# Splitting the second attention's weights once, in the first feed-forward network, and fetching the parts from DRAM twice

## The chip, the cores and the metric

The kernel runs on one core of a Trainium2 chip. The metric is the time of one execution on the device in microseconds (us); the number compared is the median over runs.

## What is computed

Two transformer blocks, the output of the first being the input of the second. The change touches the second block alone, which works on L = 512 + 16 rows (16 "meta" rows) of width 1024:

```python
for layer in range(DEPTH_2):                      # 2 layers
    h = rms_norm_2(hs, norm_mix_pre[layer])
    if layer < N_A_LAYERS:
        mix = pool_mixer(h, pool_w[layer], pool_scale[layer])
    else:
        mix = sliding_window_attention(h, k_blk, v_blk, w_q[j], b_q[j], w_o[j], b_o[j], ...)
    hs = hs + rms_norm_2(mix, norm_mix_post[layer])
    h = rms_norm_2(hs, norm_ffn_pre[layer])
    hs = hs + rms_norm_2(swiglu(h, w_gate_up[layer], w_down[layer]), norm_ffn_post[layer])
    if layer == N_A_LAYERS - 1:
        kv_in = rms_norm_2(hs, kv_norm)
        k = kv_in @ w_k + b_k;  v = kv_in @ w_v + b_v
```

So the order of the work is: pooling mixer, first network (`swiglu`, hidden width 2816), attention with `w_k`, `w_v`, `w_q`, `w_o`, second network. All is float32.

## The kernel before, in words

Everything described here is in the class `Rest`, which runs the end of the first block and all of the second, and in `Stream`, which brings its weights. TensorE (PE) takes float32r operands. To keep float32 accuracy each weight and each activation is split in two float32r parts, hi (the rounded value) and lo (the remainder), and each product is three matmuls: hi by hi, hi by lo, lo by hi (`Net.mm3`). Activations are split once, where they are made.

Weights are split on the way. `Stream.plan` (method `Rest.plan`) lists them in the order of use as *units* of 128 x 2048 values (1 MB). `Stream.load` issues a unit's DMA on SP's queue into one of RAW = 2 buffers `raw`. `Stream.conv` makes *parts* of 128 x 1024 values of it: ScalarE (ACT) writes `whi`, VectorE (DVE) then `wlo`, into rings of RING = 4 buffers each. For `w_q`, `w_k` and `w_v` both instructions multiply by a norm's gain (`gq`, `gkv`). `take` hands the next part to the matmuls, `free` gives its place in the ring back, and `pump` then queues what has become possible: a load when the unit two before it is wholly converted, a conversion when fewer than 4 parts are between it and the oldest one in use.

```python
    RING, RAW = 4, 2
            if u < len(self.units) and (u < self.RAW or self.left[u - self.RAW] == 0):
                self.todo.append((None, None, lambda u=u: self.load(u)))
            elif j < len(self.order) and self.order[j][0] < u and j - self.n_free < self.RING:
                self.todo += self.conv(j)
```

The instruction order on every engine is fixed when the program is built. `Clock` reckons when each engine would be free; `Rest.turn` puts *sides* (generators such as `heads`, one for 128 queries and 4 heads of the attention) between the matmuls of the *main* sequence where the reckoned clock has passed their due time. Where `Clock` reckons that PE waits over 0.5 us for an operand, `Engine.warm` (line 1219) puts transposes of the identity in front, one for each 0.214 us of the reckoned wait. Each engine executes its queue in order.

The main sequence around the change: `up` and `down` of the first network alternate over hidden columns, in groups of 8, 8 and 6 tiles of 128. `down(f0, f1)` takes 8 parts, one for 128 output columns (below: a *column step*), and runs the matmuls of two row halves (256 and 272) on it. The last group runs `down` twice, once for each row half, and its weights are loaded twice. Then `kv` and `q` run for rows 256 and up, then for rows 0 to 255, so `w_k`, `w_v` (0.5 MB each) and `w_q` (4 MB) are loaded and split twice. `o_proj` runs for tiles 3 and 2, then for 0 and 1, and takes `w_o` (4 MB) each time in two halves of 4 parts. For tiles 0 and 1 it waits (`until`) for all their `heads`, of which at most two are under way.

Of the kernel before, what the change touches and what calls it, by code (L numbers as in the profile page):

```python
# [11 lines left out]
F32 = mybir.dt.float32  # L12
F32R = mybir.dt.float32r
# [7 lines left out]
P = 128  # L21
# [3 lines left out]
KC = D // P  # L25
# [6 lines left out]
U = 2048  # L32
# [17 lines left out]
class Rows:  # L50


    def __init__(self, net, ats):
        self.net, self.nc, self.ats = net, net.nc, ats
# [1220 lines left out]
class Stream:  # L1275
# [3 lines left out]
    def __init__(self, net, nc, clock):  # L1279
        self.net, self.nc, self.pool, self.clock = net, nc, net.wp, clock  # L1280
        self.units, self.order = [], []
        self.raw, self.left, self.live, self.ready = {}, {}, {}, {}
        self.todo = deque()
        self.n_load = self.n_conv = self.n_take = self.n_free = self.low = 0

# [16 lines left out]
    def add(self, *units):  # L1302

        for i in range(max(len(u) for u in units)):
            self.order += [u[i] for u in units if i < len(u)]

    def pump(self):

        while True:
            u, j = self.n_load, self.n_conv  # L1310
            if u < len(self.units) and (u < self.RAW or self.left[u - self.RAW] == 0):
                self.todo.append((None, None, lambda u=u: self.load(u)))
                self.n_load += 1
            elif j < len(self.order) and self.order[j][0] < u and j - self.n_free < self.RING:
                self.left[self.order[j][0]] -= 1
                self.todo += self.conv(j)
                self.n_conv += 1
            else:
                break
# [59 lines left out]

    def take(self, n):  # L1380
        out = []
        for _ in range(n):
            while self.n_take not in self.live:
                self.tick(1)
            out.append(self.live[self.n_take])
            self.n_take += 1
        return out

# [7 lines left out]
class Rest:  # L1396
# [463 lines left out]
        if keys:  # L1860
            self.until(*keys)

    def plan_down(self, lay, f0, f1):
        wdn = self.a["w_down"][lay].rearrange("(fc p) n -> p fc n", p=P)
        for dq in range(4):
            self.st.add(self.st.unit(wdn[:, f0:f1, 256 * dq:256 * dq + 256], f1 - f0, 256, "col"))

    def down(self, f0, f1, cols, act, yT, first):
        for c in range(KC):
# [101 lines left out]

        return at

    def plan_kv(self):
        for nm in ("w_k", "w_v"):
            self.st.add(self.st.unit(self.a[nm].rearrange("(kc p) n -> p kc n", p=P), KC, P, fix=self.scaled("gkv")(0)))

    def plan_q(self):
        wq = self.a["w_q"].rearrange("(kc p) n -> p kc n", p=P)
        for u in range(4):  # L1980
            self.st.add(self.st.unit(wq[:, :, 256 * u:256 * u + 256], KC, 256, fix=self.scaled("gq")(0)))

    def window_consts(self):
        nc, a = self.nc, self.a
# [180 lines left out]
    def plan(self):  # L2165
        self.plan_rows(self.a["w_ple_gate"], self.scaled("gp"))
        for lay, plan_down in ((0, self.plan_down), (1, self.plan_down_tokens)):
            for f in (0, 2, 0, 2, 4, 6):
                self.plan_up(lay, f)
            plan_down(lay, 0, 8)  # L2170
            for f0, f1 in self.groups:
                for f in range(f0, f1, 2):
                    self.plan_up(lay, f)
                plan_down(lay, f0, f1)
            if lay == 0:
                self.plan_down(0, 16, 22)
                for i in range(2):
                    self.plan_kv()
                    self.plan_q()
                for i in range(2):  # L2180
                    self.plan_rows(self.a["w_o_2"])

    def run(self, y2, proj):
        nc, a, net, st = self.nc, self.a, self.net, self.st
# [196 lines left out]
```

## Time and profile before

| | us |
|---|---|
| median of 3 runs | 1947.39 (1944.37 to 1947.91) |
| the profiled execution | 1945.09 |
| its span (first to last instruction) | 1943.3 |
| PE busy in it | 1890.7 (97%) |
| DVE busy, ACT busy | 813.4, 662.9 |

The span is what the views of the trace divide up; 1.8 us of the execution's time lie around it. PE's matmuls are pipelined, so "busy" does not mean that it runs at its peak rate. PEclk is the clock granted to TensorE as a share of its upper level of 2.4 GHz; 0.50 is the lower level, 1.2 GHz. SPq is SP's queue, which issues the DMAs; an issue's time to landing is from its issue to its last byte.

### The profile page before, as it was taken

What the parts mean: (1) busy time and instruction counts of PE and PEld (TensorE: products, weight loads), DVE (VectorE), ACT (ScalarE), POOL (GpSimd) and SP (SyncE); (2) the same over time, 40 slices, a digit from 0 to 9 for tenths busy, and PEclk for the clock granted to TensorE, in tenths of its full rate; (3) what the DMA queues carried; (4) which work ended last, traced back from release to release, by engine and by line L of the source; (5) the groups of instructions that cost most, each with busy time, mean ns of one, the idle gap of its engine ahead of it and who ended that gap; (6) DMA issues with size and microseconds to landing.
All of it is one profiled execution on the core that took longest, in us unless ns stands there. A gap on an engine that the chain in (4) does not pass through costs nothing.

```text
span 1943.3 us, 27812 instructions
## 1 busy us (share of the span) xinstructions
PE 1890.7 (97%) x11322; PEld 1473.8 (76%) x11322; DVE 813.4 (42%) x1740; ACT 662.9 (34%) x1394; POOL 107.1 (6%) x183
## 2 busy tenths in 40 slices
PE   9998999999999999988999999999999899999998
PEld 7766888855445445437899999999987598888886
DVE  5577334411111111118565323334897774233334
ACT  4333333221111111116464333223787663333232
POOL 2100000020000000001101000000100000000000
PEclk9999999999999999999999999999999899999999
DMA  7222236589999999995035322223433144223322
GB/s 191 87 87 65 85 103 238 215 356 384 417 417 417 418 417 417 419 400 212 23 109 178 110 94 88 87 88 98 146 126 109 66 157 158 87 90 106 108 76 76
DMA packets 182101, 365.58 MB, mean 188 GB/s; under 512 B 25909, under 2 KB 127925, under 8 KB 162514
## 3 DMA queue, kind: packets, MB, share of 16 engines
q1 hardware_dynamic: 178834, 357.47, 50.1%
q0 software_dynamic: 2560, 4.20, 0.6%
q8 instruction: 90, 1.47, 0.3%
q10 hardware_dynamic: 576, 2.10, 0.3%
q14 instruction: 41, 0.34, 0.1%
HBM read 355.34 MB, written 12.58 MB: 189 GB/s over the span
## 4 chain that ended last, share of the span: by engine, by line
PE 49%; issue 21%; DVE 3%; ACT 2%; POOL 2%; DMA 1%; POOLq 0%; DVEq 0%; ACTq 0%; another core or an unknown queue 0%; SPq 0%
PE acc L1206 46%; PE tmp L1206 3%; POOL y L128 1%; DVE wlo L1206 1%; DVE h L1206 1%; ACT whi L1206 1%; DMA act<-y 0%; DVE big L1206 0%; DMA raw<-in_w_q_dram 0%; ACT junk L1206 0%; ACT big L1206 0%; DMA y<-ys,si 0%; DVE x L1206 0%; DVE y L1206 0%; ACT kt L1206 0%
## 5 line engine op out<-in xcount | busy, mean ns | idle before, releaser
L1206 PE MATMUL acc<-x,whi 128*128 128x256 f32 (+2 forms) x2560 | 539.2, 308 | 0.1
L1206 PEld LDWEIGHTS acc<-x,whi 128*128 128x128 f32 x2560 | 414.2, 189 | 25.9 <-issue 2.6
L1206 PE MATMUL acc<-x,wlo 128*128 128x256 f32 (+2 forms) x1280 | 392.7, 307 | 0.0
L1206 DVE TENSOR_TENSOR wlo<-raw,whi 128x512 fp32r<-128x512 f32 (+1 forms) x348 | 224.9, 688 | 311.3 <-ACT whi L1206 310.0
L1206 ACT ACTIVATE whi<-raw 128x512 fp32r<-128x512 f32 (+1 forms) x348 | 196.1, 615 | 325.5 <-PE acc L1206 270.2
L1206 PEld LDWEIGHTS acc<-x,wlo 128*128 128x128 f32 x1280 | 242.6, 190 | 11.2
L104 DVE TENSOR_TENSOR hd<-acc,sl 64x512 f32<-64x512 f32 x32 | 34.0, 1061 | 345.2 <-ACT sl L101 345.2
L1206 PE MATMUL acc<-whi,act 128*128 128x512 f32 x480 | 152.0, 392 | 0.0
L71 PEld LDWEIGHTS tmp<-one,n 128*128 128x128 f32 x1024 | 116.7, 192 | 25.2 <-issue 25.1
L1206 PE MATMUL acc<-act,whi 128*128 128x256 f32 (+1 forms) x704 | 131.3, 287 | 0.6 <-ACT act L1206 0.5
L96 PE MATMUL acc<-wide,xT 128*64 128x512 f32 x544 | 124.4, 596 | 0.0
L71 PE MATMUL tmp<-one,n 128*128 128x128 f32 x1024 | 122.5, 278 | 1.5 <-DVE one L61 1.5
L234 PE MATMUL acc<-wide,whi 128*128 128x512 f32 x288 | 115.6, 401 | 0.0
L236 PE MATMUL acc<-wide,wlo 128*128 128x512 f32 x288 | 112.5, 391 | 0.0
L235 PE MATMUL acc<-wide,whi 128*128 128x512 f32 x288 | 112.2, 389 | 0.0
L1206 PEld LDWEIGHTS acc<-act,whi 128*128 128x128 f32 x704 | 110.1, 190 | 1.1 <-ACT act L1206 0.7
L230 DVE TENSOR_TENSOR wlo<-raw,whi 128x1024 fp32r<-128x1024 f32 x56 | 68.0, 1222 | 92.6 <-ACT whi L227 92.5
L1206 PEld LDWEIGHTS acc<-whi,act 128*128 128x128 f32 x480 | 90.2, 188 | 20.0 <-issue 1.4
L1206 PE MATMUL acc<-act,wlo 128*128 128x256 f32 (+1 forms) x352 | 100.6, 286 | 0.0
L1206 PE MATMUL acc<-wlo,act 128*128 128x512 f32 x240 | 93.5, 389 | 0.0
L125 ACT COPY ys<-acc 128x512 f32<-128x512 f32 x32 | 18.8, 586 | 214.6 <-PE acc L119 214.6
L96 PEld LDWEIGHTS acc<-wide,xT 128*64 128x64 f32 x544 | 37.2, 137 | 67.5 <-issue 65.1
(449 smaller groups left out, 2599.8 us busy)
## 6 DMA issues: line engine op xcount, KB each, us to landing
wide<-in_w_dram SPq DMA_DIRECT2D x90, 1024.0 KB, 15.2
ew<-in_w_dram SPq DMA_DIRECT2D x62, 1024.0 KB, 20.1
raw<-in_w_gate_up_dram SPq DMA_DIRECT2D x52, 1024.0 KB, 5.2
raw<-in_w_in_dram SPq DMA_DIRECT2D x20, 1024.0 KB, 5.6
raw<-in_w_down_dram SPq DMA_DIRECT2D x18, 1024.0 KB, 5.1
raw<-in_w_o_dram SPq DMA_DIRECT2D x12, 1024.0 KB, 5.1
raw<-in_w_q_dram SPq DMA_DIRECT2D x8, 1024.0 KB, 5.2
raw<-in_w_down_dram SPq DMA_DIRECT2D x8, 768.0 KB, 4.5
```

The costliest lines, as they stand in the source:

```text
L71: self.nc.tensor.matmul(self.ps[:, k % 4], self.net.n2[t][:, k * P:(k + 1) * P], self.one[:, t].rearrange("p j s -> p (j s)"), start=t == ...
L96: self.nc.tensor.matmul(self.ps[SL * i:SL * i + SL], x, w(r), start=kc == 0, stop=kc == KC - 1)
L104: self.nc.vector.tensor_tensor(self.hd[SL:].rearrange("q fc p -> q p fc"), v(self.ps[SL:]), v(sl[SL:]), OP.mult)
L125: self.nc.scalar.copy(self.ys, self.py)
L128: return self.nc.gpsimd.indirect_dma_start(out=self.y2.rearrange("r (h d) -> (r h) d", h=2), out_offset=bass.IndirectOffsetOnAxis(ap=self. ...
L230: self.nc.vector.tensor_tensor(lo, x, hi.bitcast(F32), OP.subtract)
L234: mm(out, l[0], r[0], start=start, stop=False)
L235: mm(out, l[0], r[1], start=False, stop=False)
L236: mm(out, l[1], r[0], start=False, stop=stop)
L1206: r = f(*a, **k)
```

## The change

`plan_down` pairs each of its 1 MB units of the first network with a unit of the attention: `w_q` (4 units) with the first group, `w_o` (4) with the second, `w_k` and `w_v` with the third (its first pass). The parts alternate in the order, so of the 4 places in the ring and of the 2 `raw` buffers half go to them. When `take` comes to such a part it issues two DMAs of 512 KB that write it to a DRAM tile of its own (`put`), and its place is free when the next part is taken. In the attention the order then holds entries without a unit (`again`): `fetch` reads the two halves of a part from DRAM straight into `whi` and `wlo`. 18 parts are written once and read twice.

```diff
+    def store(self, unit, beside):
+        j = len(self.order)
+        self.add(beside, unit)
+        own = [i for i in range(j, len(self.order)) if self.order[i][0] == unit[0][0]]
+        for i in own:
+            self.ahead[i] = len(self.kept)
+            self.kept.append(None)
+        return [self.ahead[i] for i in own]
+
+    def again(self, parts):
+        self.order += [(None, k) for k in parts]
+
+    def put(self, j):
...
+            self.nc.sync.dma_start(d, x.bitcast(F32))
...
+        self.gone.add(j)
+
+    def fetch(self, j):
+        self.live[j] = t = []
+        for tag, d in zip(("whi", "wlo"), self.kept[self.order[j][1]]):
+            x = self.pool.tile([P, U // 2], F32R, tag=tag, bufs=self.RING, name=f"{tag}{j}")
...
+            self.nc.sync.dma_start(x.bitcast(F32), d)
     def pump(self):
+        while self.n_free in self.gone:
+            del self.live[self.n_free]
+            self.n_free += 1
...
+            elif j < len(self.order) and self.order[j][0] is None and j - self.n_free < self.RING:
+                self.todo.append((None, None, lambda j=j: self.fetch(j)))
+                self.n_conv += 1
     def take(self, n):
...
+            if self.n_take in self.ahead:
...
+                self.put(self.n_take)
...
+                self.pump()
+            else:
+                out.append(self.live[self.n_take])
-    def plan_down(self, lay, f0, f1):
+    def plan_down(self, lay, f0, f1, beside=()):
...
+            if dq < len(beside):
+                kept += self.st.store(beside[dq](), u)
+            else:
+                self.st.add(u)
     def plan(self):
...
+            beside = [[x] for x in (self.units_q(), self.units_o(), self.units_kv())] if lay == 0 else [[]] * 3
+            kept = [plan_down(lay, 0, 8, *beside[0])]
...
                 for i in range(2):
-                    self.plan_kv()
-                    self.plan_q()
+                    self.st.again(kept[2])
+                    self.st.again(kept[0])
                 for i in range(2):
-                    self.plan_rows(self.a["w_o_2"])
+                    self.st.again(kept[1])
```

Three places show how the instructions move. First ACT's queue in `down(0, 8)`, around the fifth and sixth of its eight column steps. `COPY y<-acc` is the eviction of one row half of a column step, `whi<-raw` the hi half of a conversion (2 or 4 instructions for one part), `gq` the gain that marks a part of `w_q`. Before:

```order
L1206 COPY y_7900<-acc_8148 128x256
L1206 COPY y_7900<-acc_8182 128x272
L1206 ACTIVATE whi_8212<-raw_8052 128x512 x2
L1206 COPY y_7900<-acc_8208 128x256
L1206 COPY y_7900<-acc_8240 128x272
L1206 ACTIVATE whi_8270<-raw_8170 128x512 x2
```

Now:

```order
L1206 COPY y_7902<-acc_8194 128x256
L1206 ACTIVATE whi_8201<-raw_8113,gq 128x256
L1206 ACTIVATE whi_8243<-raw_8084 128x512 x2
L1206 ACTIVATE whi_8260<-raw_8113,gq 128x256 x2
L1206 COPY y_7902<-acc_8226 128x272
L1206 ACTIVATE whi_8260<-raw_8113,gq 128x256 x2
L1206 COPY y_7902<-acc_8272 128x256
L1206 COPY y_7902<-acc_8306 128x272
L1206 ACTIVATE whi_8336<-raw_8258 128x512 x2
L1206 COPY y_7902<-acc_8342 128x256
L1206 ACTIVATE whi_8395<-raw_8294,gq 128x256 x3
```

Each column step now has two conversions instead of one. Before, the parts made here (`whi_8212`, `whi_8270`) are weights of the next `up`; now `whi_8243` and `whi_8336` are the next column step's own weights: `acc_8342`, whose eviction follows `whi_8336`, is computed with it.

Second, SP's queue in the same stretch (`raw_8084` and `raw_8258` are the third and fourth unit of `w_down`, `kept` the tiles in DRAM). Before it held only loads, `raw_7802` being the third unit of `w_down`:

```order
L1206 DMA raw_7802<-in_w_down_dram 128x8x256 [waits DMAHW1_49,DVE_49]
L1206 DMA raw_7928<-in_w_down_dram 128x8x256 [waits DMAHW5_49,DMAHW2_49,DVE_49]
L1206 DMA raw_8052<-in_w_gate_up_dram 128x8x256 [waits DMAHW4_49,DVE_49]
```

Now:

```order
L1206 DMA raw_8084<-in_w_down_dram 128x8x256 [waits DMAHW4_49,DVE_49]
L1206 DMA raw_8113<-in_w_q_dram 128x8x256 [waits DMAHW5_49,DMAHW3_49,DVE_49]
L1206 DMA kept_0_8128<-whi_8015 128x1024
L1206 DMA kept_1_8130<-wlo_8016 128x1024
L1206 DMA kept_0_8190<-whi_8086 128x1024 [waits DMAHW6_49]
L1206 DMA kept_1_8192<-wlo_8087 128x1024 [waits DMAHW7_49]
L1206 DMA raw_8258<-in_w_down_dram 128x8x256 [waits DMAHW2_49,DMAHW0_49,DVE_49]
```

A unit of `w_down` now alternates with one of `w_q`, and four writes of 512 KB stand between two of them.

Third, PE's queue where `o_proj` of tiles 3 and 2 ends and that of 0 and 1 begins (`acc<-whi,act` is `o_proj`; `kt`, `big` and `pt` mark the three matmul steps of a side `heads`; `dg` a norm's transpose). Before, after the last matmul of tile 2:

```order
L1206 MATMUL acc_12788<-whi_12687,act_260_11235 128x512
L1206 MATMUL tmp_12876<-ident,big_11236 128x128 x4
L1206 MATMUL tmp_12883<-ident,big_11236 128x128 x4
L1206 MATMUL acc_12897<-pt_12875,meta_11238 64x256 x2
L1206 MATMUL acc_12897<-pt_12882,meta_11238 64x256 x2
L1206 MATMUL acc_12903<-kt_7096,y_11993 128x256
L1206 MATMUL acc_12904<-kt_7096,y_11993 128x256
...
L1206 MATMUL tmp_13028<-ident,big_11236 128x128 x4
L1206 MATMUL acc_13038<-whi_12811,act_257_11232 128x512
```

Now, from the last matmul of tile 2:

```order
L1206 MATMUL acc_12999<-whi_12857,act_258_11507 128x512
L1206 MATMUL acc_13075<-whi_13022,act_255_11504 128x512
L1206 MATMUL acc_13075<-wlo_13024,act_255_11504 128x512
L1206 MATMUL acc_13075<-whi_13022,act_256_11505 128x512
L1206 MATMUL tmp_13080<-ident,big_11508 128x128 x4
L1206 MATMUL acc_13075<-whi_13022,act_255_11504 128x512
```

Before, 22 instructions of sides with two more `kt` steps stood between the two passes of `o_proj`; now the next pass follows at once and all `kt` steps lie ahead of tile 2's last matmuls.

## Rows read from the trace of the kernel before

**Rows 1.** The page: busy time by engine (us, share of the span, instructions).

```profile
PE 1890.7 (97%) x11322; PEld 1473.8 (76%) x11322; DVE 813.4 (42%) x1740; ACT 662.9 (34%) x1394; POOL 107.1 (6%) x183
```

**Rows 2.** Stretch, length; PE, PEld, DVE, ACT, POOL busy; PEclk, DMA share, GB/s.

```profile
1084.80:1138.00 53.20, 53.20 (x437) 53.20 (x436) 13.72 (x22) 17.55 (x39) 0.00 (x0) 1.00 0.25 80
1385.00:1405.00 20.00, 17.33 (x146) 16.70 (x145) 16.77 (x40) 18.55 (x49) 2.01 (x4) 1.00 0.60 200
1405.00:1485.00 80.00, 78.26 (x639) 67.56 (x638) 68.78 (x266) 62.38 (x186) 1.22 (x2) 1.00 0.35 110
1520.00:1545.00 25.00, 16.17 (x91) 11.88 (x91) 20.30 (x69) 15.24 (x45) 2.05 (x5) 0.80 0.24 85
```

**Rows 3.** PE from 1520 us, in order of time: start, us, what, [idle before <-releaser].

```profile
1520.22 1.46 PE L1206 MATMUL tmp<-ident,big 128*128 128x128 f32 x8
1527.89 1.97 PE L1206 MATMUL acc<-pt,meta 128*64 128x256 f32 x8 [6.21 <-ACT pt L1206]
...
1536.20 3.68 PE L1206 MATMUL tmp<-dg,h 128*128 128x128 f32 x16 [1.90 <-ACT pt L1206]
...
1558.28 0.61 PE L1206 MATMUL acc<-whi,act 128*128 128x512 f32 x2
...
1558.96 0.61 PE L1206 MATMUL acc<-whi,act 128*128 128x512 f32 x2
```

**Rows 4.** The same columns in three short stretches around waits of PE.

```profile
970.00:976.00 6.00, 6.00 (x27) 5.80 (x27) 2.66 (x7) 2.52 (x7) 0.74 (x2) 0.50 0.01 3
1388.00:1394.00 6.00, 4.69 (x41) 4.55 (x40) 5.02 (x12) 5.29 (x14) 0.55 (x1) 1.00 0.88 280
1528.00:1532.00 4.00, 4.00 (x17) 2.04 (x18) 3.27 (x8) 0.70 (x2) 0.55 (x1) 0.50 1.04 393
```

**Rows 5.** `w_q`'s conversions, 1370 to 1563 us: count, busy us, mean ns, idle before.

```profile
L1206 ACT ACTIVATE whi<-raw,gq 128x256 fp32r<-128x256 f32 x64 | 27.4, 498 | 3.1 <-PE acc L1206 1.6 <-DMA raw<-in_w_q_dram 1.5
L1206 DVE SCALAR_TENSOR_TENSOR wlo<-raw,gq,whi 128x256 fp32r<-128x256 f32 x64 | 27.3, 478 | 1.5 <-ACT whi L1206 1.4
```

**Rows 6.** ACT and DVE in a column step of `down(0, 8)`, in order of time.

```profile
1117.48 0.39 ACT L1206 COPY y<-acc 128x272 f32<-128x272 f32 x1 [2.66 <-PE acc L1206]
1117.77 1.15 ACT L1206 ACTIVATE whi<-raw 128x512 fp32r<-128x512 f32 x2
...
1118.43 1.29 DVE L1206 TENSOR_TENSOR wlo<-raw,whi 128x512 fp32r<-128x512 f32 x2 [4.61 <-ACT whi L1206]
```

**Rows 7.** DMA issues: count, KB each, median us from issue to landing.

```profile
raw<-in_w_down_dram SPq DMA_DIRECT2D x18, 1024.0 KB, 5.1
raw<-in_w_down_dram SPq DMA_DIRECT2D x8, 768.0 KB, 4.5
raw<-in_w_pc_dram SPq DMA_DIRECT2D x4, 512.0 KB, 3.5
```

**Rows 8.** The page: GB/s moved, in 40 slices of the span.

```profile
GB/s 191 87 87 65 85 103 238 215 356 384 417 417 417 418 417 417 419 400 212 23 109 178 110 94 88 87 88 98 146 126 109 66 157 158 87 90 106 108 76 76
```

**Rows 9.** ACT in the third `down`, one conversion a column step; PE's warm transposes (L1219).

```profile
1358.66 0.94 ACT L1206 ACTIVATE whi<-raw 128x384 fp32r<-128x384 f32 x2 [0.69 <-PE acc L1206]
1360.92 0.94 ACT L1206 ACTIVATE whi<-raw 128x384 fp32r<-128x384 f32 x2 [1.32 <-PE acc L1206]
...
1443.62 0.71 PE L1219 MATMUL tmp<-ident 128*128 128x128 f32 x5
```

**Rows 10.** Who PE waited for, 1340 to 1600 us: total us, times, longest.

```profile
PE acc L1206 <- ACT pt L1206: 6.5, 2, 6.2
PE tmp L1206 <- ACT pt L1206: 2.6, 2, 1.9
PE tmp L1206 <- ACT row L1206: 1.7, 2, 1.1
PE tmp L1206 <- DVE x L1206: 1.3, 1, 1.3
```

**Rows 11.** Who PE waited for, 950 to 1000 us.

```profile
PE tmp L1206 <- DVE x L1206: 1.7, 1, 1.7
```

More of the change, by code (lines that the diff above doesn't have):

```diff
@@ L1282, in __init__ @@
         self.raw, self.left, self.live, self.ready = {}, {}, {}, {}
+        self.ahead, self.kept, self.gone = {}, [], set()
         self.todo = deque()
@@ L1305, in add @@
             self.order += [u[i] for u in units if i < len(u)]
+    def store(self, unit, beside):
[9 more added lines that the diff above has]
+    def put(self, j):
+        t = self.live[j]
+        out = []
+        for x in t:
+            k = self.ahead[j]
+            d = self.net.dram.tile([P, U // 2], F32, name=f"kept{k}_{len(out)}")
+            d = d[:, :x.shape[1] * x.shape[2]].rearrange("p (a b) -> p a b", a=x.shape[1])
+            self.nc.sync.dma_start(d, x.bitcast(F32))
+            out.append(d)
+        self.kept[k] = out
+        self.gone.add(j)
[3 more added lines that the diff above has]
+            x = self.pool.tile([P, U // 2], F32R, tag=tag, bufs=self.RING, name=f"{tag}{j}")
+            x = x[:, :d.shape[1] * d.shape[2]].rearrange("p (a b) -> p a b", a=d.shape[1])
+            self.nc.sync.dma_start(x.bitcast(F32), d)
+            t.append(x)
     def pump(self):
+        while self.n_free in self.gone:
+            del self.live[self.n_free]
+            self.n_free += 1
         while True:
@@ L1313, in pump @@
                 self.n_load += 1
-            elif j < len(self.order) and self.order[j][0] < u and j - self.n_free < self.RING:
+            elif j < len(self.order) and self.order[j][0] is None and j - self.n_free < self.RING:
+                self.todo.append((None, None, lambda j=j: self.fetch(j)))
+                self.n_conv += 1
+            elif (j < len(self.order) and self.order[j][0] is not None and self.order[j][0] < u
+                  and j - self.n_free < self.RING):
                 self.left[self.order[j][0]] -= 1
@@ L1381, in take @@
         out = []
-        for _ in range(n):
+        while len(out) < n:
             while self.n_take not in self.live:
                 self.tick(1)
-            out.append(self.live[self.n_take])
+            if self.n_take in self.ahead:
+                was = self.clock.cur
+                self.put(self.n_take)
+                self.clock.cur = was
+                self.pump()
+            else:
+                out.append(self.live[self.n_take])
             self.n_take += 1
@@ L1861, in reach @@
             self.until(*keys)
-    def plan_down(self, lay, f0, f1):
+    def plan_down(self, lay, f0, f1, beside=()):
         wdn = self.a["w_down"][lay].rearrange("(fc p) n -> p fc n", p=P)
+        kept = []
         for dq in range(4):
-            self.st.add(self.st.unit(wdn[:, f0:f1, 256 * dq:256 * dq + 256], f1 - f0, 256, "col"))
+            u = self.st.unit(wdn[:, f0:f1, 256 * dq:256 * dq + 256], f1 - f0, 256, "col")
+            if dq < len(beside):
+                kept += self.st.store(beside[dq](), u)
+            else:
+                self.st.add(u)
+        return kept
     def down(self, f0, f1, cols, act, yT, first):
@@ L1972, in scaled, with units_kv, units_q, units_o @@
         return at
[L1974 to L1978, printed above, removed]
+    def units_kv(self):
+        return [lambda nm=nm: self.st.unit(self.a[nm].rearrange("(kc p) n -> p kc n", p=P), KC, P,
+                                           fix=self.scaled("gkv")(0)) for nm in ("w_k", "w_v")]
+    def units_q(self):
         wq = self.a["w_q"].rearrange("(kc p) n -> p kc n", p=P)
-        for u in range(4):
-            self.st.add(self.st.unit(wq[:, :, 256 * u:256 * u + 256], KC, 256, fix=self.scaled("gq")(0)))
+        return [lambda u=u: self.st.unit(wq[:, :, 256 * u:256 * u + 256], KC, 256, fix=self.scaled("gq")(0))
+                for u in range(4)]
+    def units_o(self):
+        wo = self.a["w_o_2"].rearrange("(kc p) n -> p kc n", p=P)
+        return [lambda hf=hf, u=u: self.st.unit(wo[:, 4 * u:4 * u + 4, 512 * hf:512 * hf + 512], 4, 512)
+                for hf in range(2) for u in range(2)]
     def window_consts(self):
@@ L2169, in plan @@
                 self.plan_up(lay, f)
-            plan_down(lay, 0, 8)
-            for f0, f1 in self.groups:
+            beside = [[x] for x in (self.units_q(), self.units_o(), self.units_kv())] if lay == 0 else [[]] * 3
+            kept = [plan_down(lay, 0, 8, *beside[0])]
+            for (f0, f1), x in zip(self.groups, beside[1:]):
                 for f in range(f0, f1, 2):
                     self.plan_up(lay, f)
-                plan_down(lay, f0, f1)
+                kept.append(plan_down(lay, f0, f1, *x))
             if lay == 0:
```

## The prediction

> **What bounds the kernel now.** The page comes first: PE is busy 97% of the span [rows 1], so the time changes only where PE waits, runs at its lower clock or gets more work. The busy time by stretch then shows where that is. In the downs PE is busy throughout, with ACT busy 17.6 us and DVE 13.7 us of 53.2: conversions would fit there by their size. In the stretches of kv, q and o_proj PE is idle 2.7 us of 20, 1.7 us of 80 and 8.8 us of 25, with DVE busy over 80% [rows 2]. The list of who PE waited for names evictions and copies of ACT and DVE, never a weight [rows 10]. The timeline shows the one large place: after o_proj of tiles 3 and 2 PE has only sides left, waits 6.2 us for `pt` and later 1.9 us [rows 3], and the granted clock falls to 0.50, the 1.2 GHz level [rows 4].
>
> **What the change gives back.** It takes every conversion of the attention's weights out of 1370 to 1563 us. For `w_q` alone these are 27.4 us on ACT and 27.3 us on DVE [rows 5]. On the path lies only what PE loses there: 2.7 + 1.7 + 8.8 us idle, and the clock. Its mean of 0.80 over 25 us [rows 2] is 5.0 us; about 1.9 us of the slow time was idle anyway, so half of that comes off and 4.0 us remain. Together 17.2 us. Not all returns: the sides' steps still follow each other through DVE, ACT and PE, at most two at a time. While DVE was over 80% busy and PE still had main work, PE lost 1.7 us in 80 [rows 2]; I leave twice that, 3.4 us, for the whole attention. The order supports the rest: the block of sides between the two passes of o_proj is gone. **Gain 13.8 us**, bounds 5 (the copy of `pt` stays late in other places) and 17.2.
>
> **What it costs in the downs.** The ring holds four parts, two of them now only passing through, and with two `raw` buffers a unit of `w_down` is loaded only when the one before it is wholly converted. Prices: a column step 5.9 us (1.29 + 4.61), ACT 0.58 us and DVE 0.65 us for half a part, one ACT instruction of `w_q` 0.43 us (27.4 / 64), a 1 MB load 5.1 us [rows 5 to 7].
>
> *First down*, from the start of its first column step. The second unit is wholly converted at 14.2, the third lands at about 19.4. Its first part stands behind an eviction at 20.7 and is ready in time; its second stands behind a part of `w_q` and an eviction and is ready at 29.5, just in time. Only then is the fourth loaded: 34.6. The seventh step is due at 35.4; ACT first evicts the sixth (0.4), then converts the first half (0.58), DVE follows (0.65): 37.0. PE needs lo at its third matmul, 0.24 us in, so it waits 1.5 us. The eighth step's part stands behind an eviction and a `w_q` instruction: 2.0 us. The next `up` waits for a load issued after that conversion: 1.4 us. Sum 4.9.
>
> *Second down*: the same loop, with DVE adding where ACT copied: 0.9 + 2.2 + 1.3 = 4.4.
>
> *Third down*: a column step is only 2.3 us [rows 9], a 768 KB load 4.5 us [rows 7]. The fourth step's part stands behind the eight DVE instructions of `w_v`: 1.9 us. The next load is issued behind the write of `w_v`'s part at 8.7, loses 0.9 us to it, lands at 14.1 and is converted at 14.9, due 11.1: 3.8 us. Sum 5.7.
>
> **Loss 15.0 us.** Downwards it is bounded by instructions: the order has 65 warm transposes at these eight places where before there were none, and five took 0.71 us [rows 9], so 9.1 us pass even if every weight is on time. Upwards I add 1.3 us (half a part behind a write) for each of the eight waits: 25.
>
> **What the fetches cost.** A part is two DMAs of 0.524 MB. One such load alone lands in 3.5 us [rows 7]; the bulk rate of the first block, 417 GB/s [rows 8], makes 1.26 us of each further one. In q a unit needs four, 3.5 + 3 x 1.26 = 7.3 us, and has the matmuls of the unit before plus sides, so nothing is charged. In o_proj three matmuls take 0.68 us [rows 3], a tile 5.45. The second half of `w_o` in the last pass starts to arrive when six matmuls of the tile before are done (1.4 us): first half part at 4.9, the eighth at 13.7, five matmuls after it 14.8, against 10.9 without waits: 3.9 us. At the start of that pass the lo half comes 0.5 us late, then sides give time. **Loss 4.4 us**, bounds 0.5 and 8 (the earlier sets also late). The Trainium skill (DMA: Bandwidth & Descriptors, Bandwidth) says that HBM limits such transfers to about 358 GB/s for a core. By it the last set would take 1.7 us longer and the sum be 7.3. The trace has 417 GB/s for reads and so speaks against it.
>
> Costed at nothing: the writes themselves, 18.9 MB in the downs, where DMA's share is 0.25 [rows 2]; were that cover gone, they are in the upper bound. SP's queue also carries the loads for the second network ahead of the fetches; PE has o_proj's matmuls meanwhile.
>
> **Sum**: 15.0 + 4.4 - 13.8 = +5.6 us. The profiled execution would go from 1945.1 to 1950.7; it lies 2.3 us below the median of the runs, so against that I forecast **1953.0 us**. Some 0.2%, 3.9 us, is what a measurement can tell from no change.
>
> **Rivals.**
>
> *A, the weights come in time* (ends at no change). Place: the eight waits. Each is the lateness of one loop of load, conversion and eviction, about 1.9 us on average; if loads land some 2 us sooner than 5.1 the loop fits into two column steps and only the transposes remain: 9.1 + 4.4 - 13.8 = -0.3, 1947.1 us. For it: DMA is 25% busy there, and the chain through ACT that I added up has slack at each handover. Against it: the load's time is the median of 18 [rows 7], and the waits begin only where a load follows a conversion directly. With the whole 17.2 us returned it reaches -3.7, with the fetches hidden as well -7.6.
>
> *B, the clock falls* at the new waits. After a wait of 1.7 us [rows 11] it stood at 0.50 for six busy microseconds [rows 4], a loss of 3.0; after one of 1.3 us [rows 10] at 1388 us it stayed at 1.00 [rows 4]. The transposes fill about half of each new wait, so most idle stretches would stay near 1 us. Were four of the eight to trip it: 5.6 + 12 = +17.6, 1965 us. The Trainium skill (TensorE: Matmul & The Clock Gate, HAM oscillation) describes such a loop, whose wait for the next DMA sends the array back to its lower clock each time.
>
> *C, the gap only moves.* The sides go on at two at a time, and their steps now stand closer between o_proj's matmuls; if ACT's copy of `pt` is late there, PE's queue stands still with main work behind it. With 5 us returned: +14.4, 1961.8 us. For it: the waits for `pt` are 9.1 of the 12.1 us listed [rows 10]. Against it: the conversions that delayed DVE are gone.
>
> **How the numbers follow.** Forecast 0.50, A 0.25, B 0.13, C 0.12. The forecast's own range is 1946 to 1960, from half the bounds on each side; of its chance I give 0.04 to faster, 0.16 to the same, 0.30 to slower. A gives 0.10, 0.12, 0.03; B 0, 0.02, 0.11; C 0.01, 0.01, 0.10. Sums: faster 0.15, same 0.31, slower 0.54. The range for 8 in 10 reaches down to A's better half and up into B and C: 1941 to 1964.
>
> **What would show it.** Downs: PE idle or transposing in the seventh and eighth column step and at the next up of the first two, and in the fourth and fifth of the third, 15 us more than before in all; none would mean A. Attention: no wait over 1 us and granted clock 1.00 between the passes of o_proj; waits for `pt` at several places would mean C. A wait for `wlo` by DMA in the last pass of o_proj shows the fetch term. Granted clock under 1.00 in the first network means B. I am wrong if PE waits for `w_q`'s fetches, which I charged nothing.

## The result and the profile after

The changed kernel takes 1964.8 us (median of 4 runs, 1961.55 to 1968.7), the kernel before, beside it on the same chip, 1945.88. The ratio is 1.0100 with a 95% interval of 1.0086 to 1.0114: 17 to 22 us slower. The profiled execution took 1965.63 us with a span of 1963.8.

The page of the changed kernel, to be held against [rows 1] (the last row is its account of DRAM traffic; before it stood at 355.34 MB read and 12.58 MB written):

```profile
PE 1906.3 (97%) x11385; PEld 1483.0 (76%) x11385; DVE 787.2 (40%) x1676; ACT 637.7 (32%) x1330; POOL 106.9 (5%) x183
HBM read 383.66 MB, written 31.46 MB: 211 GB/s over the span
```

PE's share is 97% again: the share hides the loss, since PE's busy time now holds 65 warm transposes and the span grew with it. The stretches below are cut where the first matmul of a stage starts: `down(0, 8)`, the second `up`, the second `down`, the third `up` and `down`, kv and q, `o_proj` (columns as in [rows 2]):

```profile
1092.06:1144.92 52.86, 50.96 (x409) 49.84 (x407) 20.22 (x43) 25.14 (x60) 0.00 (x0) 1.00 0.84 287
1144.92:1239.28 94.36, 93.49 (x769) 92.88 (x769) 36.78 (x68) 32.22 (x67) 0.00 (x0) 1.00 0.33 108
1239.28:1291.82 52.54, 49.45 (x401) 48.81 (x399) 23.71 (x45) 15.94 (x30) 0.00 (x0) 1.00 0.84 293
1291.82:1362.74 70.92, 70.26 (x576) 69.66 (x577) 28.83 (x58) 25.55 (x58) 0.00 (x0) 1.00 0.34 111
1362.74:1414.68 51.94, 49.06 (x398) 47.48 (x397) 34.02 (x77) 25.25 (x62) 4.80 (x9) 1.00 0.68 231
1414.68:1510.64 95.96, 93.36 (x752) 82.75 (x751) 50.44 (x209) 45.44 (x139) 2.58 (x6) 0.98 0.65 230
1510.64:1590.83 80.19, 73.05 (x394) 51.20 (x393) 40.88 (x158) 38.98 (x126) 3.41 (x7) 1.00 0.49 180
```

The same cuts in the kernel before (the first `down` to the end of the third; kv and q; `o_proj`):

```profile
1087.76:1392.11 304.35, 302.49 (x2490) 301.42 (x2489) 123.13 (x247) 106.01 (x234) 4.34 (x9) 1.00 0.30 97
1392.11:1488.50 96.39, 93.29 (x761) 80.95 (x759) 80.19 (x292) 76.82 (x221) 3.23 (x6) 1.00 0.38 123
1488.50:1570.06 81.56, 72.73 (x378) 54.09 (x377) 57.97 (x185) 51.57 (x150) 3.15 (x7) 0.94 0.27 91
```

The first network went from 304.3 to 322.6 us (+18.3), the attention from 178.0 to 176.2 (-1.8). DVE is busy 53% of kv and q instead of 83%, and yet the stage is as long. The other 4.4 us of this execution lie ahead of everything that the change touches: the first `up` starts anywhere from 978.9 to 985.6 us in the 17 kernels profiled here, on the same instructions. So I compare stages inside traces, and medians between kernels.

Who PE waited for, first from 1085 to 1415 us, then from 1415 to 1600 (as [rows 10]):

```profile
PE acc L1206 <- DVE wlo L1206: 4.7, 9, 1.7
PE acc L1206 <- ACT whi L1206: 4.4, 7, 1.5
...
PE acc L1206 <- DMA wlo<-kept: 3.7, 5, 0.8
PE tmp L1206 <- ACT pt L1206: 2.5, 3, 1.2
PE tmp L1206 <- ACT row L1206: 2.0, 2, 1.5
PE acc L1206 <- DMA whi<-kept: 1.0, 1, 1.0
```

The 6.2 us for `pt` of [rows 3] are gone, the weights' waits are new. Where the first kind comes from shows on ACT, second `down` (start, us, what, [idle before <-releaser]):

```profile
1259.15 1.15 ACT L1206 ACTIVATE whi<-raw 128x512 fp32r<-128x512 f32 x2 [5.51 <-DMA raw<-in_w_down_dram]
1263.89 2.19 ACT L1206 ACTIVATE whi<-raw 128x512 fp32r<-128x512 f32 x4 [3.59 <-DMA kept<-whi]
1266.33 1.16 ACT L1206 ACTIVATE whi<-raw 128x512 fp32r<-128x512 f32 x2 [0.25 <-DMA kept<-whi]
1274.16 1.15 ACT L1206 ACTIVATE whi<-raw 128x512 fp32r<-128x512 f32 x2 [6.67 <-DMA raw<-in_w_down_dram]
1279.25 3.23 ACT L1206 ACTIVATE whi<-raw 128x512 fp32r<-128x512 f32 x6 [3.94 <-DMA raw<-in_w_o_dram]
```

and beside it on SP's queue, then on PE:

```profile
1255.22 0.38 SPq L1206 DMA_DIRECT2D raw<-in_w_o_dram  x1
1255.65 0.50 SPq L1206 DMA_DIRECT2D kept<-whi  x1
...
1267.63 0.38 SPq L1206 DMA_DIRECT2D raw<-in_w_down_dram  x1
```

```profile
1276.00 0.38 PE L1206 MATMUL acc<-act,wlo 128*128 128x256 f32 x1 [0.56 <-DVE wlo L1206]
...
1281.77 0.60 PE L1219 MATMUL acc<-ident 128*128 128x128 f32 x4
1284.26 0.38 PE L1206 MATMUL acc<-act,wlo 128*128 128x256 f32 x1 [1.66 <-DVE wlo L1206]
```

Read it as a chain. ACT has nothing to do from 1260.3. The next conversion needs a unit of `w_o`, issued at 1255.22, and a place in the ring whose part is being written from 1255.65 on. The unit landed 7.3 us after its issue, at 1262.5 (the DMA issues of 1255 to 1255.5 us: count, KB, us to landing):

```profile
raw<-in_w_o_dram SPq DMA_DIRECT2D x1, 1024.0 KB, 7.3
```

The write lands last, and ACT starts at 1263.89. Behind it stands the second part of the unit of `w_down`. Only when that is converted is the next unit loaded (1267.63); ACT starts on it at 1274.16, and PE waits at 1276.00. The wait at 1284.26 comes through the next unit of `w_o`: its conversion, ahead of the second part of `w_down`, could start only at 1279.25. The prediction had this loop, but not its first link. Over the first network ACT waited five times for a write:

```profile
ACT whi L1206 <- DMA kept<-whi: 10.6, 5, 3.6
```

The DMA issues of 1085 to 1300 us show why (count, KB each, median us to landing):

```profile
...
kept<-whi SPq DMA_DIRECT2D x16, 512.0 KB, 8.7
kept<-wlo SPq DMA_DIRECT2D x16, 512.0 KB, 9.0
raw<-in_w_down_dram SPq DMA_DIRECT2D x7, 1024.0 KB, 5.0
raw<-in_w_o_dram SPq DMA_DIRECT2D x4, 1024.0 KB, 6.9
raw<-in_w_q_dram SPq DMA_DIRECT2D x3, 1024.0 KB, 8.3
```

Two column steps, 11.8 us, now carry two loads of 1 MB and four writes of 0.5 MB; the DMA share in the downs is 0.84 (0.25 before, [rows 2]). A write that met less other traffic, issued at 1283.63 us, landed in 2.8 us:

```profile
kept<-wlo SPq DMA_DIRECT2D x1, 512.0 KB, 2.8
```

By this comparison most of the 8.7 us is the company of loads and of other writes, and the place in the ring is held all that time. The Trainium skill (DMA: Bandwidth & Descriptors, Anatomy of one DMA) says, of DMAs that GpSimd issues, that one counts as complete only when its last byte is confirmed, a long delay above all where the target is HBM, and gives most of 2 us for it. The writes here go through SP's queue, and the 2.8 us leave room for such a delay but do not show it.

### The profile page after: what moved, and what is told of

The parts are those of the page before. It is cut to its first block, busy times and chain, and to the rows that moved or that the text cites. A ratio compares the mean times of both kernels' runs of the same rounds, so it can differ in the third digit from the quotient of the medians.

```text
span 1963.8 us, 27974 instructions
## 1 busy us (share of the span) xinstructions
PE 1906.3 (97%) x11385; PEld 1483.0 (76%) x11385; DVE 787.2 (40%) x1676; ACT 637.7 (32%) x1330; POOL 106.9 (5%) x183
## 4 chain that ended last, share of the span: by engine, by line
PE 70%; DMA 3%; DVE 3%; ACT 1%; issue 1%; POOL 0%; SPq 0%; DVEq 0%; ACTq 0%
PE acc L1206 46%; PE acc L96 10%; PE tmp L71 5%; PE acc L119 5%; PE tmp L1206 3%; DMA wide<-in_w_dram 1%; DMA raw<-in_w_gate_up_dram 1%; DVE wlo L1206 1%; PE acc L110 1%; DVE h L1206 1%; DMA wlo<-kept 0%; DMA raw<-in_w_ple_gate_dram 0%; ACT junk L1206 0%; DMA act<-y 0%; DVE y L1206 0%
## 5 line engine op out<-in xcount | busy, mean ns | idle before, releaser
L1206 DVE TENSOR_TENSOR wlo<-raw,whi 128x512 fp32r<-128x512 f32 (+1 forms) x332 | 213.7, 687 | 296.9 <-ACT whi L1206 294.9
L1206 ACT ACTIVATE whi<-raw 128x512 fp32r<-128x512 f32 (+1 forms) x332 | 185.6, 614 | 319.8 <-PE acc L1206 216.0
```

The source lines that it names most:

```text
L1206: r = f(*a, **k)
```

## Experiments

Theory A is the prediction's: the loop of load, conversion and eviction is late by itself. Theory B: the writes make it late, B1 by the places of the ring that they hold until they land, B2 by delaying the loads.

**The attention alone.** Nothing beside the downs (`beside = [[]] * 3`); the attention multiplies by four stand-in parts, written in the first `up`:

```diff
+            if self.n_take in self.copied:
...
+                    d = self.copies[self.copied[self.n_take]][h]
+                    self.nc.sync.dma_start(d.rearrange("p (a b) -> p a b", a=x.shape[1]), x.bitcast(F32))
...
     # in `fetch`, e1_free and e9_free2 only: fetched once, then reused
+        for x, d in zip(self.base[(j - self.first) % self.RING], pair):
+            t.append(x.rearrange("p (a b) -> p a b", a=d.shape[1]))
```

e2_fetch and e10_fetch2 keep the change's `fetch`. e9_free2 and e10_fetch2 copy 16 parts later.

> Leaves out: the attention multiplies by four parts of the first network's weights, which are fetched once into the four places of the ring and stay there; nothing is stored or converted beside the downs (the four parts are written to DRAM once, in the first up). So neither the downs nor a fetch costs anything, and what is left is the gain in the attention alone. The prediction's term (13.8 us): 1945.9 - 13.8 = 1932 us, with no wait over 1 us between the passes of o_proj. The theory from the changed kernel's trace (gain 7.8 us: the large gap goes, but waits for ACT's row and pt of some 5 us and a stretch of low clock stay): 1938 us.

> Leaves out: as in e1_free the attention multiplies by four parts of the first network's weights, and nothing is stored or converted beside the downs; but every part of the attention is fetched from DRAM as in the changed kernel (two DMAs of 512 KB). Against e1_free this is the cost of the fetches alone, against the kernel before the attention's net. Prediction's terms: +4.4 on e1_free, 1936.5 us. Theory from the trace: +6.0 on e1_free (waits for whi and wlo by DMA 4.7 us, and PE's restarts), 1944 us. If the fetches also slow the side work, more than 6 us on e1_free.

> As e1_free, but the four parts are written to DRAM some 60 us later, in the fifth pair of columns of the first up and not at its start, where the trace of e1_free has one more wait of PE (0.6 us for dg) and 13.7 us at the lower clock against 3.4 in the kernel before. If that stretch took back part of the gain: 1934 us, which is the sum of the stages that the change touches in e1_free's trace (kv and q -2.1, o_proj -8.3, the last down -2.0), near the prediction's 13.8. If the gain is 7 us: 1938 us again.

> As e2_fetch, the four parts written at the later place. With e9_free2 it gives the cost of the fetches: the stages of the two earlier traces say 7 us (o_proj 6.3, the rest elsewhere), the prediction 4.4. 1941 us if the gain is 12, 1945 us if it is 7.

Measured against 1945.38: e1_free 1938.1, e2_fetch 1944.7; against 1944.96: e9_free2 1934.55 (ratio 0.9943, 0.9930 to 0.9955), e10_fetch2 1940.2 (0.9978, 0.9968 to 0.9988). By these medians the copies at the start of the first `up` cost some 4 us. In the trace of e1_free PEclk is 0.52 from 990 to 1004 us, in the kernel before 0.88, but it is 0.88 too in e2_fetch, which has the same copies, so that the clock is the reason is not shown:

```profile
990.00:1004.00 14.00, 12.59 (x61) 12.00 (x60) 6.77 (x17) 7.53 (x17) 0.55 (x2) 0.52 0.61 250
```

So the later pair counts: gain 10.4 us, fetch 5.7. Kv and q and `o_proj` in e9_free2, and what PE still waited for there:

```profile
1392.30:1486.70 94.40, 91.80 (x752) 81.19 (x751) 50.44 (x209) 45.45 (x139) 2.58 (x6) 1.00 0.07 25
1486.70:1559.90 73.20, 71.08 (x394) 51.45 (x393) 40.85 (x158) 38.93 (x126) 3.40 (x7) 1.00 0.00 1
```

```profile
PE tmp L1206 <- ACT pt L1206: 2.1, 3, 0.9
PE tmp L1206 <- ACT row L1206: 2.0, 2, 1.5
```

Even with no conversion and no fetch, and with DVE busy only 53% of kv and q, these waits stay: they come with the sides, not with a DVE full of conversions.

**The downs alone.** The change's downs and writes, the attention as before:

```diff
-                    self.st.again(kept[2])
-                    self.st.again(kept[0])
+                    for x in self.units_kv() + self.units_q():
+                        self.st.add(x())
                 for i in range(2):
-                    self.st.again(kept[1])
+                    self.plan_rows(self.a["w_o_2"])
```

> The downs of the changed kernel, with the conversions and the writes of the attention's parts beside them, and the attention of the kernel before, which loads and splits its weights twice; the parts in DRAM are not read. Theory (the downs cost 18 us, whatever the attention does): 1945.9 + 18 = 1964 us, PE waits for wlo and whi in the downs as in the changed kernel. If the costs do not add (the attention's gap takes up what was lost before it, or the changed kernel's loss arises in the attention): under 1960 us. The prediction's term: 1961 us.

1972.55 us (1.0148, 1.0131 to 1.0164), 27 us more. First network 327.3 us, kv and q 105.1 against 96.39. The costs don't add: the third `down` alone took 56.0 us, 4 more than in the changed kernel, with the attention's own conversions close behind it. That these are the reason is not shown.

**Conversions, traffic and held places apart.** The loads and conversions beside the downs stay; the writes go (e4_noput, e13_noput2) or take rows of the residual instead of the parts (e5_traffic, e14_traffic2). The attention fetches the stand-in parts.

```diff
     def put(self, j):
...
-            self.nc.sync.dma_start(d, x.bitcast(F32))       # e4_noput, e13_noput2: no write
+            self.nc.sync.dma_start(d, self.net.h[k % 4])    # e5_traffic, e14_traffic2
```

> The changed kernel without the 36 writes: the attention's parts are converted beside the downs and dropped, and the attention fetches four parts of the first network instead (so it multiplies by other weights). Theory A (the prediction's: the loop of load, conversion and eviction is late, the writes ride along): the downs lose what they lost, at most 2 us less, 1963 us. Rival B (the writes: 18.9 MB in some 100 us of downs make the loads beside them land in 8.3 us instead of 5.1 and hold a place of the ring 9 us each): the downs' waits mostly go, 1950 us, and a load of w_q lands in about 5 us.

> As e4_noput (the attention's parts are dropped, the attention multiplies by parts of the first network), but with 36 writes of 512 KB again, from rows of the residual, which stay where they are: the same bytes at the same places of SP's queue, and no place of the ring waits for a write to land. Theory B1 (the writes cost because a place of the ring is held until they land, some 9 us): no more than e4_noput, 1951 us. Theory B2 (the writes cost because the loads of the downs stand behind them and share the DMA engines): as the changed kernel, 1965 us. In between if both take part.

> As e4_noput (conversions beside the downs, no writes), the four stand-in parts written at the later place as in e10_fetch2. The difference to e10_fetch2 (1940.2) is then what the conversions cost by themselves. By the stages of e4_noput's trace 6.6 us, nearly all in the third down: 1947 us. The prediction's loop of loads and conversions, which did not need the writes: 15 us, 1955 us.

> As e5_traffic (the same bytes written from rows that stay, no place of the ring held), the stand-in parts at the later place. The difference to e13_noput2 is what the writes cost by delaying the loads, the rest up to the changed kernel (1964.8) what they cost by holding places of the ring. By the stages of e5_traffic's trace 3 us and 15 us: 1950 us; by its median 8 us and 10 us: 1955 us.

Medians: e4_noput 1950.6, e5_traffic 1958.7; with the later copies e13_noput2 1949.4 (1.0020, 1.0011 to 1.0029) and e14_traffic2 1956.6 (1.0063, 1.0049 to 1.0076). Lengths in us, cut as above:

| | first down | up | second down | up | third down | sum |
|---|---|---|---|---|---|---|
| before | 47.2 | 92.4 | 47.2 | 69.3 | 48.2 | 304.3 |
| e10_fetch2 (nothing beside) | 47.2 | 92.4 | 47.3 | 69.2 | 47.8 | 303.9 |
| e13_noput2 (loads and conversions) | 47.2 | 93.2 | 47.3 | 69.3 | 52.3 | 309.3 |
| e14_traffic2 (and writes of other rows) | 49.7 | 96.6 | 47.2 | 70.4 | 51.4 | 315.3 |
| changed (and places held) | 52.9 | 94.4 | 52.5 | 70.9 | 51.9 | 322.6 |

So by these traces, in the first network, the conversions with their loads cost some 5 us, nearly all in the third down; the writes' traffic 6 more; the held places 7 more. The traces of e4_noput and e5_traffic give 310.9 and 313.8 us in the same cuts, which makes 7, 3 and 9; the medians of the later pair give 9, 7 and 8 for the whole kernel (the profiled execution of e13_noput2 was its fastest, 4.5 us under its median). All three are there each time; which is the largest stays open. The first and the third down in e13_noput2:

```profile
1085.90:1133.10 47.20, 47.20 (x386) 47.20 (x385) 19.67 (x41) 22.89 (x54) 0.00 (x0) 1.00 0.49 158
...
1342.90:1395.20 52.30, 48.37 (x392) 46.79 (x391) 34.16 (x77) 25.19 (x62) 4.79 (x9) 1.00 0.54 180
```

and the first and the second in e14_traffic2:

```profile
1089.10:1138.80 49.70, 47.94 (x386) 47.28 (x384) 19.31 (x40) 22.38 (x54) 0.00 (x0) 1.00 0.82 278
...
1235.40:1282.60 47.20, 47.20 (x386) 47.20 (x385) 21.91 (x42) 14.60 (x27) 0.00 (x0) 1.00 0.87 292
```

Without writes PE is busy in every microsecond of the first down, with all the conversions in it. In e14_traffic2 ACT never waits for a write's landing. Its second down loses nothing at 292 GB/s, where the changed kernel lost 5.3 us at 293: there the held places, not the DMA engines' load, are what costs. The writes of e14_traffic2 also wait for no conversion, as those of the changed kernel do, and so could hold up a load behind them in SP's queue. In the changed kernel's second down this did not happen: each load was issued within 0.1 us of the conversion that freed its buffer.

**The writes on another queue.**

```diff
-            self.nc.sync.dma_start(d, x.bitcast(F32))
+            self.nc.gpsimd.dma_start(d, x.bitcast(F32))
```

> The changed kernel, its 36 writes issued by GpSimd instead of SP, so that no load of SP's queue is issued behind them; everything is computed as before. B1 (places held until the writes land): no faster, 1965 us, more if GpSimd's writes land later. B2, if the order in SP's queue is what delays the loads: 1951 to 1957 us, and a load of w_q lands in 5 to 6 us instead of 8.3. B2, if the DMA engines' share is what delays them: as the changed kernel, 1965 us.

1980.7 us (1.0192, 1.0175 to 1.0209), 16 more than the changed kernel. The issues of 1085 to 1300 us:

```profile
...
kept<-whi POOLq DMA_DIRECT2D x15, 512.0 KB, 5.3
raw<-in_w_down_dram SPq DMA_DIRECT2D x7, 1024.0 KB, 6.7
...
raw<-in_w_q_dram SPq DMA_DIRECT2D x3, 1024.0 KB, 10.6
```

The writes land sooner (those of `wlo` in 6.6 us), the loads later, and PE waited 17.8 us for `whi` between 1085 and 1435 us. The Trainium skill (DMA: Bandwidth & Descriptors, Issuing engines are not separate DMA queues) says that DMAs of all issuing engines run on the same 16 engines and interleave, so that another queue brings no bandwidth; these rows agree.

**Without the warm transposes.**

```diff
-        if wait > IDLE:
+        if wait > IDLE and not c.cold:      # cold from the first down to kv
```

> The changed kernel without the 65 warm transposes of the first network's downs (72 to 7). If they only fill time in which PE waits anyway: 1965 us, and PE's waits for whi and wlo in the downs grow from some 9 to some 17 us. If they run on after the weights are there, as the prediction's lower bound has it: up to 9 us less, 1956 us. If they hold the clock up: the waits, 1.5 to 2.5 us now, each end in a stretch at the lower clock, up to 1977 us.

1965.8 us, no difference that the medians can tell. PE's waits from 1085 to 1415 us grew from 9.1 to 16.4 us, so the transposes had filled time that was idle anyway:

```profile
PE acc L1207 <- ACT whi L1207: 10.3, 5, 4.3
PE acc L1207 <- DVE wlo L1207: 6.1, 9, 2.1
```

They also held the clock: it is 1.00 in all downs of the changed kernel, here 0.74 from 1365 to 1385 us:

```profile
1365.00:1385.00 20.00, 13.95 (x87) 13.31 (x86) 9.91 (x25) 6.81 (x18) 0.00 (x0) 0.74 0.67 226
```

The first network takes 329.2 us, 6.6 more. In the two traces 3.8 us of that don't show, since this one reaches the first down at 1088.2 us and the changed kernel's at 1092.1; why the medians show none of it stays open.

**Other places for the same work.** One unit of the attention behind each of nine calls of `plan_up` (the two small ones, `w_k` and `w_v`, behind the last):

```diff
+            def up(f):
                 self.plan_up(lay, f)
...
+                if todo:
+                    for x in todo[:1 if len(todo) > 2 else 2]:
+                        ks.extend(self.st.alone(x()))
+                        todo.pop(0)
```

> All of the change, but the nine units of the attention stand one each behind a call of plan_up (two units of w_gate_up, then one of the attention) instead of one to one beside w_down. Conversions and writes are the same in number and bytes; per column time there are 2.1 MB of writes in 23 us instead of 11.7. If the loss in the downs was one of density (loads, writes and places of the ring within two column steps): most of the 20 us go, 1945 to 1948 us, no wait of PE for whi or wlo in the first network. If conversions or writes cost by their number, wherever they stand: 1960 to 1965 us.

1940.1 us (0.9981, 0.9966 to 0.9995): all writes and conversions are there, and the loss is gone. From 1085 to 1400 us PE waited for no weight. Its first `up` took 110.6 us, though, against 107.1 in the kernel before, with a wait of 2.0 us for `big` (0.5 before) and PEclk 0.77 from 990 to 1000 us; whether the units that now lie there are the reason is not shown. The stretches of the first and the second down and of the `up` between them:

```profile
1092.10:1139.90 47.80, 47.49 (x386) 47.27 (x385) 13.69 (x22) 16.94 (x37) 1.10 (x2) 1.00 0.39 131
1139.90:1232.30 92.40, 92.40 (x770) 92.40 (x769) 41.00 (x82) 38.50 (x84) 0.00 (x0) 1.00 0.63 216
1232.30:1279.60 47.30, 47.30 (x387) 47.30 (x386) 20.20 (x38) 11.52 (x22) 0.00 (x0) 1.00 0.35 118
```

Then two parts of each pass of `w_o` in the idle `raw` buffers:

```diff
+        if j in self.in_raw:
+            raw = self.pool.tile([P, U], F32, tag="raw", bufs=self.RAW, name=f"raw_{j}").bitcast(F32R)
...
+    def raw_free(self, u):    # e12_best, e15_best2: > max(self.in_raw) + 2; e15_best2: a fetch goes first
+        k = u - self.u_again
+        return k < 0 or self.n_free > sorted(self.in_raw)[-2 if k == 0 else -1]
```

> e7_ups, and four fetched parts of w_o (the first two of each pass) go to the two raw buffers, which are free during the attention, so that two parts of the second half of w_o are fetched while the first half is in use; the second network's first loads wait for these buffers. If the fetch term (6.6 us between e1_free and e2_fetch) is the late second half: 4 to 6 us less than e7_ups, some 1940 us, faster than the kernel before. If the second network's first weights come late in its place: no gain on e7_ups or a loss of up to 5 us.

> e8_upsraw with two things moved: the second network's first loads are let go only when the second half of w_o is on its way (in e8_upsraw they stood ahead of it in SP's queue and PE waited 4.0 us for whi), and the attention's units stand behind the calls of plan_up from the second group of columns on, w_k and w_v behind the first down, not in the first 90 us of the up. If the late second half is the fetch term and nothing is late behind it: 1936 us, 10 less than the kernel before. If the second network's first weights are now late: 1940 us or more, with a wait for whi at the start of its first up.

> e12_best with one change: where a fetch and a load are both possible, the fetch is issued first. In e12_best the last part of w_o stood behind two loads of the second network and PE waited 6.5 us for whi. If the fetch term is the late second half alone: this wait goes, 1936 to 1938 us, 2 to 4 less than e7_ups. If the last part is late anyway, by its own 3.5 us and the wait for its place: 1940 us or more.

e8_upsraw 1942.3, e12_best 1943.4 (0.9995, 0.9986 to 1.0004), e15_best2 1938.7 (0.9968, 0.9956 to 0.9980). In the first two PE waited once for a part that stood behind the second network's loads on SP's queue (4.0 us in e8_upsraw; e12_best:)

```profile
1563.54 0.79 PE L1206 MATMUL acc<-whi,act 128*128 128x512 f32 x1 [6.45 <-DMA whi<-kept]
```

With the fetch issued first that wait is gone and only 1.9 us for `wlo` are left. e15_best2 is the fastest version that does all of the kernel's work, 6 us faster than the kernel before; its lead over e7_ups is within what their intervals leave open.

## Why the prediction was off

The sign and the stages were right, the size was not: +5.6 us expected, +18.9 measured, 0.8 us outside the range.

**The step that failed** is "Costed at nothing: the writes themselves, 18.9 MB in the downs, where DMA's share is 0.25". The share was that of the kernel without them. From the change's own list the step could have been worked out: in 11.8 us two loads and four writes, 4.2 MB, are 355 GB/s beside the 417 of [rows 8]. The trace has 287 to 293 GB/s in the first two downs at a DMA share of 0.84. The Trainium skill (DMA: Bandwidth & Descriptors, Bandwidth) gives some 358 GB/s for a core, which I had weighed for the fetches alone; by it the downs would be full. Busy engines alone do not make PE wait, as the second down of e14_traffic2 shows. The second effect was in the code: a place is free only when its write has landed. By the traces of e13_noput2 and e14_traffic2 the writes cost 13.3 us (6.0 traffic, 7.3 held places), by those of e4_noput and e5_traffic 11.7, by the medians 15.4.

**Loss in the downs, 15.0 forecast, 18.3 found**, but not by the working. *First and second down*, 4.9 and 4.4 by the loop: PE waits where the prediction put it, in the seventh and eighth column step (around 1129, 1137, 1276 and 1284 us) and at the next `up`. Yet without the writes these waits are gone: the loop alone costs 0.0 and 0.1 us in these downs and 0.8 and 0.0 in the `up` behind them (e13_noput2). A load of `w_q` takes 7.9 us in that kernel, not 5.1, and is in time all the same; rival A was right about the loop in these two downs and wrong only because it left the writes out too. The 7.6 and 7.0 us found in the two downs with their next `up` have another cause than the 4.9 and 4.4 forecast: that place and sum came out near is luck. *Third down*, 5.7: 3.7 in the changed kernel, 4.1 without the writes, with the waits in its fourth and fifth column step; there the mechanism held, at two thirds of its size. *The lower bound* of 9.1 us from 65 transposes was none: they are put where the planner reckons a wait, 22 remain without the writes, and taking all away saved nothing. Rival B's 1965 us is the measured time, but by luck: the granted clock was 1.00 in all three downs.

**Gain, 13.8 forecast, 10.4 found** (e9_free2, 8.8 to 13.6 by its interval). Of 8.8 + 4.0 us at the gap 8.3 came back. Of 2.7 + 1.7 us in kv and q only 2.0 did: 1.5 us for `row` stay. "I leave twice that, 3.4 us" put these waits down to a busy DVE. In the changed kernel the attention returned 2.0 us less still (176.2 against 94.1 + 80.1 in e10_fetch2): after that wait of 1.5 us PEclk was 0.63 from 1424 to 1428 us, which is rival B at a place where I had not looked for it. The same wait in e10_fetch2 left it at 1.00, so the wait's length alone does not decide it. In the changed kernel, then in e10_fetch2:

```profile
1423.68 0.44 PE L1206 MATMUL tmp<-ident,row 128*128 128x128 f32 x2 [1.50 <-ACT row L1206]
1424.00:1428.00 4.00, 3.72 (x21) 3.60 (x20) 2.32 (x7) 1.15 (x2) 0.76 (x3) 0.63 0.64 257
...
1399.36 0.44 PE L1206 MATMUL tmp<-ident,row 128*128 128x128 f32 x2 [1.49 <-ACT row L1206]
1400.00:1404.00 4.00, 3.93 (x34) 3.93 (x35) 2.24 (x7) 1.75 (x3) 0.74 (x2) 1.00 0.41 162
```

Rival C did not come: waits for `pt` fell from 9.1 to 2.5 us.

**Fetch, 4.4 forecast, 5.7 to 6.6 found** (by the medians; by the two stages, 174.2 us in e10_fetch2 against 167.6 in e9_free2). The last set waited 3.9 us in five places, just as worked out with 417 GB/s, the start of the pass 0.8 instead of 0.5. The rest lies outside these waits: in `o_proj` of e10_fetch2 PE is busy 2.1 us longer than in e9_free2 (73.2 against 71.1) and waits once 1.0 us for `st`, both for reasons not shown. The 1.7 us more that the 358 GB/s of the Trainium skill (DMA: Bandwidth & Descriptors, Bandwidth) would have added are not needed for the waits. Nothing waited for `w_q`'s fetches, as charged.

Put together: 18.3 + 6.6 - 10.4 + 2.0 = 16.5 us, against 17 to 22 by the interval. This is the difference of the two traces' stages (18.3 - 1.8) in other words, not a check on it.

## What to carry to other kernels

When work is moved under a cover, check the cover for every resource the work uses, with the work already in it: ACT, DVE and PE had room in the downs, the ring had none, and the DMA engines had little. A buffer that is written out is occupied until the write lands, some 9 us here, and whatever is queued in order behind the next use of that buffer waits too. The same work beside the calls of `up`, at half the density, made PE wait for no weight from the first down on; whether the other place or the lower density did it, no run here separates.

## What the hardware showed that I had not expected

Writes of 512 KB landed in 8.7 to 9.0 us on SP's queue between loads (2.8 for one with less beside it) and in 5.3 to 6.6 on GpSimd's, where the loads paid for it (10.6 instead of 8.3 us). The clock's low stretches at the start of the first `up` differ in length between kernels that execute the same instructions there (PEclk 0.52 in e1_free and 0.88 in e2_fetch from 990 to 1004 us) and shift whole executions by some us, so a single trace can't price 5 us. Transposes in idle time cost nothing that the medians show, and with them the granted clock stayed at 1.00 through waits of up to 1.7 us in the downs (0.74 in one stretch without them).
